# Weight sums of the seven-product down projection: from GpSimd to VectorE

## The chip, the cores and the metric

One core of a Trainium2 chip runs the whole kernel in one launch. The metric is the device time in microseconds (us), and lower is better. Five engines take part: TensorE (PE, with its weight loads as PEld), VectorE (DVE), ScalarE (ACT), GpSimd (POOL) and SyncE (SP), which issues the transfers.

## The reference, cut to what matters

The kernel computes a two-layer decoder trunk on 512 tokens of width 1024. Layer 0 has stick-breaking attention and layer 1 sliding-window attention. Each of them stands between two half-step SwiGLU blocks, so there are four SwiGLU blocks (stages 0, 1, 2 and 3), each with weights of its own:

```python
def swiglu(h, w_gate_up, w_down):
    gate, up = jnp.split(h @ w_gate_up, 2, axis=-1)
    return (jax.nn.silu(gate) * up) @ w_down

x = x + 0.5 * swiglu(rms_norm(x, norm_gains[i, 0]), ffn_w_gate_up[i, 0], ffn_w_down[i, 0])
```

The hidden width is 2816, which is 22 tiles of 128. Only the second product, with `w_down`, has to do with the change.

## The kernel before, in words

**Layout and precision.** Activations are kept transposed, as tiles of 128 features by 512 tokens. Every float32 operand of a matmul is split into a high and a low part (`hi`, `lo`), and each product is made of three matmuls. The weights come from HBM as float32 into `raw` buffers (two rings, three buffers in a feed-forward stage: `raw`, `raw`, `rawx`), issued by SyncE. They are split into `slot` buffers (four, each with room for 6 tiles of 128x128): ScalarE casts the high part (L282), VectorE subtracts to get the low part (L287).

**A feed-forward stage.** It has two halves, of 6 and of 5 pairs of hidden tiles (`PAIRED`). A half first makes its gate and up tiles (`gu`, 24 or 20 units of 24 matmuls with 512 columns), and `swiglu` turns each into the activation `h`. Then `down` multiplies these with the down weights.

**The seven products.** `down` works in 4 blocks. A block covers two output tiles (rows n and n+4) and takes the hidden tiles by even and odd, and the tokens by their two halves. A block is thus a 2x2 product of quarters, done with seven products in place of eight. The seven need sums of the activation quarters (`t`, L444 and L450 to L452 on VectorE, then split into `ops` at L435 and L436) and four sums of the weight quarters (`s`), which `make_sums` forms: s0 = a21+a22, s1 = s0-a11, s3 = a12-s1, s2 = a11-a21. Each has 128 rows and 6x128 or 5x128 columns. They are split like other weights (`slot<-s`). There is one buffer for each of s0 to s3, so a block's sum can't be written before the same sum of the block before has been split, and the two loads of the block must have landed.

**Order of the products.** For a block n it is 1, 5, (4 of block n-1), 2, 6, 3, 7, and the last block ends with 7, 3, 4. One product is 18 matmuls of 256 columns in the first half, and 15 in the second. The results gather in four PSUM banks (`dna` twice, `dnb`, `dnc`), and after each product VectorE adds the bank to the residual `x` (L542). Some products write again into the bank that the one before has left, so they wait for that addition. In the second half of stages 0 to 2 `norm_tile` follows on each output tile: casts and squares on ScalarE, `xl` on VectorE (L370), and the running sum of squares `acc` (L378), which GpSimd adds for 6 of 8 tiles.

**Order on the engines.** TensorE runs in the order of the program. On the other engines the compiler's scheduler sets a fixed order when the program is built: it plays the program through with its own estimates and takes, where several instructions are ready, the earlier one in the program. On the chip each engine then works strictly in that order. `pump` issues the next load as soon as a `raw` buffer is free, splits the next weights as soon as a slot is free, and calls `make_sums` when the first product of a block is next to be split, which is just behind the split for product 7 of the block before:

```python
        if column is not None and column not in self.sums:
            if self.fp and column + 1 < len(self.raws) and not self.unsplit:
                self.make_sums(column, t)
```

Of the kernel before, what the change touches and what calls it, by code (L numbers as in the profile page):

```python
# [131 lines left out]
class _Trunk:  # L132
# [76 lines left out]
    def make_sums(self, g, t):  # L209

        nc = self.nc
        a11, a12 = (self.raws[g][:, h * t * P : (h + 1) * t * P] for h in range(2))
        a21, a22 = (self.raws[g + 1][:, h * t * P : (h + 1) * t * P] for h in range(2))
        s = [self.fp.tile([P, SLOT], F32, tag=f"s{j}", name=f"s{j}_{g}", bufs=1)[:, : t * P] for j in range(4)]
        nc.gpsimd.tensor_add(s[0], a21, a22)  # L215
        nc.gpsimd.tensor_sub(s[1], s[0], a11)
        nc.gpsimd.tensor_sub(s[3], a12, s[1])
        nc.gpsimd.tensor_sub(s[2], a11, a21)
        self.sums[g] = s
        self.unsplit = 4  # L220
        self.reads[g] -= 1
        self.reads[g + 1] -= 1
# [1033 lines left out]
```

## Time and profile before

| | |
|---|---|
| median of 3 runs | 1956.06 us (1954.71 to 1960.08) |
| the profiled execution, its own time | 1953.03 us |
| its span in the profile | 1951.3 us |
| mean granted TensorE clock | 0.982 |
| PE busy | 1871.1 us |
| DVE busy | 1376.7 us |
| ACT busy | 830.7 us |
| POOL busy | 439.5 us |

In the views of the profile, times are in us from the start of the span unless marked ns. A row of the timeline has its start, its duration, the engine, the line of the kernel, the operation with output and inputs, the count, and in brackets the idle time ahead of it and what ended it. A row of the stretches has the stretch, its length, the busy time of PE, PEld, DVE, ACT and POOL with the counts of instructions, then the granted clock, the share of DMA time and the GB/s.

### The profile page before, as it was taken

The numbers are of one execution on the slowest core, as the hardware profiler recorded it, in microseconds if no ns is written. First come the engines' busy times: TensorE is split into PE (matmuls) and PEld (weight loads), VectorE is DVE, ScalarE is ACT, GpSimd is POOL, SyncE is SP. The second block draws the span as 40 slices with busy tenths as digits, with TensorE's granted clock in tenths as the row PEclk, the third lists the DMA queues.
The fourth block names the chain that finished last, engine by engine and source line by source line (L and its number), as shares of the span: only waits on it lengthen the run. The fifth ranks groups of instructions, "written<-read, shape, count | busy, mean of one in ns | idle before, by whom it ended". The sixth has DMA issues, their size and how long they took to land.

```text
span 1951.3 us, 26890 instructions
## 1 busy us (share of the span) xinstructions
PE 1871.1 (96%) x10578; PEld 1629.2 (83%) x10578; DVE 1376.7 (71%) x2208; ACT 830.7 (43%) x1384; POOL 439.5 (23%) x275
## 2 busy tenths in 40 slices
PE   9999999899999999999989999998999899999999
PEld 7889888877887888988888889888887788889889
DVE  6568557867887756856786577558877665685676
ACT  5333333456665433333343333334457543333332
POOL 1015002743321001500240033004242110131023
PEclk9999999999999999999999999998989999999999
DMA  5221322221112322132232223232210032222322
GB/s 173 98 95 68 122 95 81 89 69 56 42 65 71 114 97 97 67 120 97 72 105 97 95 73 111 95 99 76 88 60 28 18 123 97 98 80 97 105 71 98
DMA packets 36414, 170.78 MB, mean 88 GB/s; under 512 B 4416, under 2 KB 5184, under 8 KB 36288
## 3 DMA queue, kind: packets, MB, share of 16 engines
q1 hardware_dynamic: 36288, 169.07, 25.7%
q8 instruction: 83, 1.36, 0.3%
q14 instruction: 43, 0.35, 0.1%
HBM read 166.96 MB, written 2.10 MB: 87 GB/s over the span
## 4 chain that ended last, share of the span: by engine, by line
PE 80%; DVE 13%; ACT 3%; issue 3%; DMA 1%; POOL 0%; SPq 0%; ACTq 0%; DVEq 0%; POOLq 0%
PE gu L85 48%; PE dna L85 11%; PE dnc L85 4%; PE op L85 4%; DVE slot L287 4%; PE tok L85 3%; PE dnb L85 2%; PE pv L85 1%; DVE keep L640 1%; PE k L85 1%; DVE x L542 1%; DVE ops L436 1%; PE sc L85 1%; PE z L85 1%; ACT slot L282 1%
## 5 line engine op out<-in xcount | busy, mean ns | idle before, releaser
L85 PE MATMUL gu<-xh,slot 128*128 128x512 f32 x2800 | 868.2, 390 | 0.5 <-DVE slot L287 0.4
L85 PEld LDWEIGHTS gu<-xh,slot 128*128 128x128 f32 x2800 | 526.5, 188 | 112.1 <-DVE slot L287 2.1
L85 PE MATMUL gu<-xl,slot 128*128 128x512 f32 x1400 | 546.1, 390 | 2.1 <-DVE xl L370 2.1
L287 DVE TENSOR_TENSOR slot<-raw,slot 128x768 fp32r<-128x768 f32 (+2 forms) x270 | 288.1, 1068 | 165.1 <-ACT slot L282 162.7
L282 ACT CAST slot<-raw 128x768 fp32r<-128x768 f32 (+2 forms) x308 | 241.4, 785 | 363.9 <-PE gu L85 227.2
L85 PE MATMUL dna<-ops,slot 128*128 128x256 f32 x2112 | 284.4, 291 | 44.4 <-DVE x L542 31.4
L85 PEld LDWEIGHTS dna<-ops,slot 128*128 128x128 f32 x2112 | 271.8, 199 | 50.9 <-issue 25.5
L85 PEld LDWEIGHTS gu<-xl,slot 128*128 128x128 f32 x1400 | 263.5, 188 | 57.7 <-DVE xl L370 3.1
L215 POOL TENSOR_TENSOR s<-raw 128x768 f32<-128x768 f32 (+1 forms) x24 | 44.2, 1842 | 1047.0 <-DMA raw<-in_w_dram 991.6
L287 DVE TENSOR_TENSOR slot<-rawx,slot 128x768 fp32r<-128x768 f32 (+1 forms) x112 | 128.6, 1148 | 74.6 <-ACT slot L282 73.9
L282 ACT CAST slot<-s 128x768 fp32r<-128x768 f32 (+1 forms) x128 | 99.9, 781 | 145.4 <-PE dna L85 85.1
L287 DVE TENSOR_TENSOR slot<-s,slot 128x768 fp32r<-128x768 f32 (+1 forms) x128 | 143.4, 1120 | 24.3 <-ACT slot L282 23.5
L282 ACT CAST slot<-rawx 128x768 fp32r<-128x768 f32 (+1 forms) x112 | 87.0, 777 | 140.7 <-PE gu L85 78.4
L85 PE MATMUL dnc<-ops,slot 128*128 128x256 f32 x1056 | 141.4, 289 | 0.0
L85 PEld LDWEIGHTS dnc<-ops,slot 128*128 128x128 f32 x1056 | 135.7, 198 | 0.0
L285 POOL TENSOR_TENSOR slot<-raw,slot 128x384 fp32r<-128x384 f32 x76 | 91.7, 1233 | 139.5 <-ACT slot L282 139.5
L431 DVE TENSOR_TENSOR h<-gu,rbc 128x512 f32<-128x512 f32 x87 | 59.8, 688 | 83.5 <-PE gu L85 83.5
L85 PE MATMUL tok<-slot,xh 128*128 128x256 f32 x576 | 113.1, 295 | 0.2 <-POOL slot L285 0.2
L85 PEld LDWEIGHTS tok<-slot,xh 128*128 128x128 f32 x576 | 91.8, 196 | 3.1 <-issue 0.8
L430 ACT ACTIVATE g<-g 128x512 f32<-128x512 f32 x88 | 55.5, 631 | 86.6 <-DVE g L429 86.6
L435 ACT CAST ops<-h 128x256 fp32r<-128x256 f32 x88 | 45.2, 513 | 95.6 <-DVE h L432 95.6
L429 DVE TENSOR_TENSOR g<-gu,rbc 128x512 f32<-128x512 f32 x88 | 60.5, 687 | 35.9 <-PE gu L85 35.8
(303 smaller groups left out, 2503.5 us busy)
## 6 DMA issues: line engine op xcount, KB each, us to landing
raw<-in_w_dram SPq DMA_DIRECT2D x66, 768.0 KB, 4.3
raw<-in_w_dram SPq DMA_DIRECT2D x64, 640.0 KB, 3.9
rawx<-in_w_dram SPq DMA_DIRECT2D x28, 768.0 KB, 4.2
rawx<-in_w_dram SPq DMA_DIRECT2D x32, 640.0 KB, 3.9
raw<-in_ws_dram SPq DMA_DIRECT2D x20, 768.0 KB, 4.3
raw<-in_ww_dram SPq DMA_DIRECT2D x10, 768.0 KB, 4.2
x<-in_xt_dram SPq DMA_DIRECT2D x8, 256.0 KB, 5.6
out_dram<-x SPq DMA_DIRECT2D x8, 256.0 KB, 2.0
```

The lines of the kernel that those rows point to most:

```text
L85: return self._tc.keep_in_program_order(method(*args, **kwargs))
L215: nc.gpsimd.tensor_add(s[0], a21, a22)
L282: self.nc.scalar.copy(hi, src)
L285: self.nc.gpsimd.tensor_sub(lo[:, h], src[:, h], hi[:, h])
L287: self.nc.vector.tensor_sub(lo, src, hi)
L429: nc.vector.tensor_mul(g, gu[0], self.rbc)
L430: nc.scalar.activation(g, g, AF.Silu)
L431: nc.vector.tensor_mul(hf, gu[1], self.rbc)
L435: nc.scalar.copy(hi[:, a:b, :], src)
L436: nc.vector.tensor_sub(lo[:, a:b, :], src, hi[:, a:b, :])
L542: self.nc.vector.scalar_tensor_tensor(x, ps, 0.5, x, ALU.mult, ALU.add)
L640: nc.vector.tensor_tensor_scan(rev, rev, rev, 1.0, ALU.mult, ALU.bypass)
```

## The change

The four instructions of `make_sums` are issued to VectorE and not to GpSimd. Operands, shapes, buffers and their place in the program stay as they are.

```diff
-        nc.gpsimd.tensor_add(s[0], a21, a22)
-        nc.gpsimd.tensor_sub(s[1], s[0], a11)
-        nc.gpsimd.tensor_sub(s[3], a12, s[1])
-        nc.gpsimd.tensor_sub(s[2], a11, a21)
+        nc.vector.tensor_add(s[0], a21, a22)
+        nc.vector.tensor_sub(s[1], s[0], a11)
+        nc.vector.tensor_sub(s[3], a12, s[1])
+        nc.vector.tensor_sub(s[2], a11, a21)
```

There are 4 stages with 2 halves of 4 blocks, so `make_sums` runs 32 times and 128 instructions move.

## The prediction

> **What bounds the kernel now.** I read the page first, then the stretches of the eight down projections, then the timeline of one of them engine by engine, and at last who waits for whom.
>
> ```profile
> span 1951.3 us, 26890 instructions
> PE 1871.1 (96%) x10578; PEld 1629.2 (83%) x10578; DVE 1376.7 (71%) x2208; ACT 830.7 (43%) x1384; POOL 439.5 (23%) x275
> PE 80%; DVE 13%; ACT 3%; issue 3%; DMA 1%; POOL 0%; SPq 0%; ACTq 0%; DVEq 0%; POOLq 0%
> ```
>
> TensorE is the bound: busy for 96% of the span, 80% of the chain that ended last. GpSimd is on that chain with 0%, so nobody on the path waits for its results. What the change can win must come from VectorE's 13%. The next rows are stretches: first one gate and up phase, then the eight down projections from the first `dna` matmul to the next kind of matmul.
>
> ```profile
> 647.00:779.00 132.00, 132.00 (x587) 109.26 (x587) 87.85 (x178) 49.37 (x75) 9.62 (x4) 1.00 0.29 98
> ```
>
> ```profile
> 145.16:210.91 65.75, 61.16 (x505) 60.61 (x504) 54.65 (x62) 24.30 (x30) 27.05 (x12) 1.00 0.27 93
> 319.74:381.29 61.55, 53.31 (x421) 52.18 (x420) 54.17 (x65) 27.77 (x41) 34.52 (x21) 0.97 0.24 79
> ...
> 954.82:1019.17 64.35, 56.32 (x421) 54.84 (x420) 56.80 (x68) 29.27 (x44) 31.12 (x17) 0.92 0.25 78
> ...
> 1327.02:1390.88 63.86, 55.55 (x421) 54.66 (x420) 57.34 (x68) 29.41 (x44) 30.23 (x17) 0.92 0.24 78
> ...
> 1889.98:1947.67 57.69, 54.25 (x421) 53.22 (x419) 45.36 (x59) 19.34 (x27) 21.99 (x12) 0.94 0.25 88
> sum 513.05, PE 466.70 PEld 459.96 DVE 430.10 ACT 202.99 POOL 225.67; mean PE 58.34 PEld 57.49 DVE 53.76 ACT 25.37 POOL 28.21
> ```
>
> In the gate and up phase PE is busy all the time, with VectorE at two thirds. In the down projections PE idles 513.05 - 466.70 = 46.3 us. Of that the 5-pair halves have 8.2, 8.0, 8.3 and 3.4 us (length less PE busy), and the four 6-pair halves the rest, 18.3 us, 4.6 us each. The stretches are also the place where VectorE is nearly full: 57.34 of 63.86 us. Now one 6-pair half, VectorE first, then GpSimd, then PE.
>
> ```profile
> 148.17 2.07 DVE L450 TENSOR_TENSOR t<-h,t 128x256 f32<-128x256 f32 x1
> 150.16 2.06 DVE L451 TENSOR_TENSOR t<-h 128x256 f32<-128x256 f32 x1
> 152.15 0.41 DVE L452 TENSOR_TENSOR t<-h,t 128x256 f32<-128x256 f32 x1
> ...
> 153.68 0.94 DVE L436 TENSOR_TENSOR ops<-t,ops 128x768 fp32r<-128x768 f32 x1
> 154.55 0.41 DVE L542 SCALAR_TENSOR_TENSOR x<-dnc,x 128x256 f32<-128x256 f32 x1
> 154.89 2.27 DVE L287 TENSOR_TENSOR slot<-s,slot 128x768 fp32r<-128x768 f32 x1
> 157.08 0.41 DVE L542 SCALAR_TENSOR_TENSOR x<-dnb,x 128x256 f32<-128x256 f32 x1
> 157.41 2.44 DVE L287 TENSOR_TENSOR slot<-raw,slot 128x768 fp32r<-128x768 f32 x1
> 159.78 0.41 DVE L542 SCALAR_TENSOR_TENSOR x<-dna,x 128x256 f32<-128x256 f32 x1
> ```
>
> ```profile
> 147.60 2.35 POOL L215 TENSOR_TENSOR s<-rawx 128x768 f32<-128x768 f32 x1 [10.70 <-DMA rawx<-in_w_dram]
> 150.03 1.91 POOL L216 TENSOR_TENSOR s<-s,raw 128x768 f32<-128x768 f32 x1
> 153.90 2.44 POOL L217 TENSOR_TENSOR s<-raw,s 128x768 f32<-128x768 f32 x1 [1.96 <-DVE slot L287]
> 157.23 1.80 POOL L218 TENSOR_TENSOR s<-raw,rawx 128x768 f32<-128x768 f32 x1 [0.89 <-DVE slot L287]
> ```
>
> ```profile
> 152.95 2.41 PE L85 MATMUL dna<-ops,slot 128*128 128x256 f32 x18 [1.16 <-DVE x L542]
> 155.20 2.32 PE L85 MATMUL dnc<-ops,slot 128*128 128x256 f32 x18
> 160.34 1.90 PE L85 MATMUL dna<-ops,slot 128*128 128x256 f32 x14 [2.82 <-DVE x L542]
> ```
>
> Compare the two L450/L451 rows with L452, the same shape: 2.07 and 2.06 us against 0.41. They ran just while GpSimd ran a sum. Likewise the two splits of 2.27 and 2.44 against 0.94 for 768 columns. Only VectorE instructions with both inputs in SBUF are stretched; L542, which reads a bank, stays at 0.41 inside GpSimd's 153.90 to 156.34. So the two engines take turns, and GpSimd's sums hold VectorE up. PE stands for 1.16 and 2.82 us behind additions to `x` that stood in that queue.
>
> **What moves, and its price on VectorE.** 128 instructions leave GpSimd, half of 768 columns and half of 640. No transfer moves and SP's queue keeps its instructions. On VectorE the price is the step from one start to the next, since a next instruction starts before the row ends: 153.68 to 154.55 is 0.87 us for 768, and for 640 the rows below give 333.53 to 334.27, 0.74 us. A group of four costs 3.48 or 2.96 us, all 32 groups 16 x 3.48 + 16 x 2.96 = 103 us.
>
> The Trainium skill, VectorE: DVE Perf Modes, section on the TRN2 errata, gives a float32 tensor_tensor as (N+151)/0.96 ns, 957 and 824 ns here; by it all groups would cost 114 us. The rows of duration agree (0.94), but the steps are shorter, and I keep the steps.
>
> **Start of a 6-pair half.** What goes from VectorE's queue between 148.17 and 159.78: 1.66 + 1.65 (L450, L451 less 0.41) and 1.33 + 1.50 (splits less 0.94), 6.14 us. What comes is the group, 3.48 us. The chain to the addition that PE awaits gets 2.66 us shorter if all four sums stand ahead of it; if they fall into holes, both stalls go, 3.98 us at most. I take 3.3, nearer the middle since some of the sums will find holes while ScalarE makes casts: 4 x 3.3 = 13 us (10.6 to 15.9).
>
> **Start of a 5-pair half.**
>
> ```profile
> 331.14 2.14 DVE L287 TENSOR_TENSOR slot<-raw,slot 128x640 fp32r<-128x640 f32 x1
> ...
> 333.53 0.81 DVE L287 TENSOR_TENSOR slot<-s,slot 128x640 fp32r<-128x640 f32 x1
> 334.27 0.41 DVE L542 SCALAR_TENSOR_TENSOR x<-dnc,x 128x256 f32<-128x256 f32 x1
> ...
> 335.47 0.75 DVE L370 SCALAR_TENSOR_TENSOR xl<-x,gain,xh 128x512 fp32r<-128x512 f32 x1
> ...
> 349.72 1.78 DVE L370 SCALAR_TENSOR_TENSOR xl<-x,gain,xh 128x512 fp32r<-128x512 f32 x1
> ```
>
> Stage 3 has no norm behind it and idles 3.44 us, some 0.6 of it at its end (product 7 there follows 6 in one bank, which the change leaves). So its start costs 2.8, and I use this for all four. Lock waits here are 2.14 - 0.81 = 1.33 each; four of them less 2.96 leave 2.4. I take 4 x 2.4 = 10 us (6 to 11.2).
>
> **Later blocks of a 5-pair half, stages 0 to 2.** They idle 8.2 - 3.4 = 4.8 us more each, 14.4 together. Here `xl` (1.78 against 0.75, a wait of 1.03) and GpSimd's `acc` come in. Per block GpSimd holds VectorE up to six times, 6 x 1.2 (between 1.03 and 1.33) = 7.2 us; afterwards it is 2 x 1.03 + 2.96 = 5.0. That saves 2.2 us a block, but with VectorE this full it reaches PE only in part: 2 us a half, 6 together (0 to 12).
>
> **Slow matmuls behind the stalls.** From the chain of waits, in two halves:
>
> ```profile
> 160.34 4.54 PE dna L85 x36
> 164.88 2.16 PE dnc L85 x18
> ```
>
> ```profile
> 794.09 5.89 PE dna L85 x36
> ```
>
> 18 matmuls in 2.16 us are the normal pace, 0.12 each. The 36 behind a stall took 4.54 and 5.89 in place of 4.32. All 4 x (504 + 420) down matmuls at 0.12 make 443.5 us, and PE was occupied 466.7. These 23 us stand mostly behind stalls, in stretches with a granted clock of 0.92 to 0.97. With over half of the stalls gone I count 40%, 9 us (0 to 18); I don't take the full share, as two stalls of one length left such different tails.
>
> **What is late next: the loads.** From the view of L215, what ended GpSimd's idle time ahead of it (us, times):
>
> ```profile
>   DMA raw<-in_w_dram: 991.6, 18
> ```
>
> GpSimd came to its group early and sat until a load landed, 18 times by this view. GpSimd can afford it. In VectorE's queue a sum that stands there too early stops splits, activations and additions behind it, and PE behind these. The scheduler puts the sum where it estimates the landing; the trace of before can't show how good that is. Bounds: no wait, or a whole load, 4.3 us by the page's median below, per group.
>
> ```profile
> raw<-in_w_dram SPq DMA_DIRECT2D x66, 768.0 KB, 4.3
> ```
>
> A 6-pair block has 7 x 2.16 = 15.1 us of PE time, and VectorE's work then is 7 x (0.87 + 0.33) + 3.48 = 11.9, so 3.2 us are free. A 5-pair block has 12.6 against 7 x (0.74 + 0.33) + 2 x 0.75 + 2.96 = 12.0. I take a small wait, 0.3 us for each of the twelve later 5-pair groups: -4 us. The eight first groups of the halves lie in the gate and up phase, where VectorE has a third free: nothing, unless a wait there exceeds the lead of the four slots. Buffers come free no later, since the group ends earlier than GpSimd's 159.03.
>
> **The sum.** 13 + 10 + 6 + 9 - 4 = 34 us. Against the profiled execution's 1953.03 that is 1919; the median of the runs shown stands 3.0 us above it, so I predict 1956.06 - 34 = 1922 us.
>
> **Rivals.**
> *VectorE becomes the bound in the 5-pair halves.* With the `acc` waits, 12.0 + 2 x 1.03 = 14.1 us of work stand against 12.6 of PE. For: VectorE is at 57.34 of 63.86 already. Against: that figure contains waits that go. Then the later blocks win nothing, most slow tails stay, and the 5-pair starts win half: 13 + 5 - 2 = 16, 1940 us. The Trainium skill, Perfetto Trace Analysis, section Optimizing Scalar/DVE Operations, advises offloading a saturated VectorE even to GpSimd, which speaks for this rival, and adds that the shared port may spoil it, which speaks against; the rows above show the spoiling.
>
> *The sums wait for loads at the head of VectorE's queue: slower.* With a whole 4.3 us wait in 24 later groups, 6-pair blocks lose 4.3 - 3.2 = 1.1 and 5-pair blocks 4.3 - 0.6 = 3.7: 12 x 1.1 + 12 x 3.7 = 58, less the starts' 23, gives +35, 1991 us. It decides from a wait w with 12 (w - 0.6) > 23 + 6, that is about 3 us. For: most groups are gated by a load. Against: the scheduler counts some time for a load, and the start of a half has higher-ranked work to run first.
>
> *It is hidden anyway:* the order changes so that other additions to `x` come late and the stalls only move, within 6 us of 1956. Against: the lock waits on the chain exceed the sums at every place where PE stalled.
>
> **How the numbers follow.** The forecast (gain 20 to 50 us) has 0.60, a larger gain 0.04, VectorE as the bound (gain 6 to 20) 0.15, no change 0.09, slower by waits for loads 0.12. 0.3%, 5.9 us, is what a measurement of this kernel can tell, so faster 0.79, same 0.09, slower 0.12. The range 1898 to 1958 leaves out the slower rival and part of the largest gain; the forecast's own is 1906 to 1936.
>
> **What would show it.** Right: in the 6-pair halves PE's idle time falls from 4.6 to 0.6 to 2 us, L450 and L451 stand at 0.41 everywhere, splits of 768 columns at 0.94, the sums at about 0.95 and 0.82, and VectorE's total goes up by less than 103 us. The 5-pair halves of stages 0 to 2 fall from about 8 to 3 to 5 us of idle PE, and the clock there rises above 0.92. Wrong: VectorE idle for microseconds until a load ends ahead of L215, or PE waiting for `x` at more places than before.

## The result, and the profile after

The changed kernel takes 1939.76 us, the median of 4 runs (1937.73 to 1941.38), against 1955.6 for the kernel before (4 runs, 1954.71 to 1960.08). The ratio is 0.9914, with a 95% interval of 0.9896 to 0.9932: faster by 0.9%. That is inside the range of 1898 to 1958 us, but outside the 1906 to 1936 of the forecast itself, and less than half of the 34 us that were predicted. The page of its profile begins thus, with the shares of the chain as the third line here:

```profile
span 1935.8 us, 26732 instructions
...
PE 1865.5 (96%) x10578; PEld 1625.3 (84%) x10578; DVE 1342.6 (69%) x2336; ACT 833.8 (43%) x1384; POOL 174.8 (9%) x147
...
PE 77%; DVE 16%; ACT 3%; issue 2%; DMA 2%; POOL 0%; SPq 0%; ACTq 0%; DVEq 0%; POOLq 0%
```

VectorE took over 103 us of sums (the prediction's price) and is nevertheless busy for 34 us less: 1342.6 against 1376.7. So about 137 us of its busy time before (34 and 103) were waits for GpSimd. But VectorE's share of the chain went up, from 13% to 16%. The stretches of the down projections show where the gain stands (the 6-pair halves of stages 1 and 2 are left out):

```profile
145.01:208.51 63.50, 61.16 (x506) 60.63 (x505) 49.99 (x74) 24.38 (x30) 0.00 (x0) 1.00 0.29 97
317.33:379.38 62.05, 54.30 (x422) 53.57 (x420) 49.88 (x77) 29.27 (x43) 11.64 (x10) 0.94 0.23 78
...
949.08:1010.75 61.67, 54.27 (x422) 53.54 (x421) 52.60 (x80) 29.68 (x44) 7.64 (x5) 0.94 0.24 80
...
1315.09:1378.17 63.08, 55.68 (x421) 54.95 (x420) 52.16 (x80) 29.78 (x44) 7.63 (x5) 0.92 0.24 79
1702.40:1765.60 63.20, 61.02 (x505) 60.61 (x504) 50.09 (x74) 24.39 (x30) 0.00 (x0) 1.00 0.28 97
1874.43:1932.07 57.64, 52.97 (x421) 52.03 (x419) 42.58 (x71) 19.43 (x27) 0.00 (x0) 0.97 0.25 87
sum 498.26, PE 461.68 PEld 456.58 DVE 397.27 ACT 205.72 POOL 26.91; mean PE 57.71 PEld 57.07 DVE 49.66 ACT 25.71 POOL 3.36
```

The eight stretches shrank from 513.05 to 498.26, 14.8 us, nearly the whole change of the span (15.5). The four 5-pair halves sum to 244.4 us, against 247.5 before; the four 6-pair halves to 253.8 against 265.6. So the 6-pair halves gave 11.8 us and the 5-pair halves 3.0. PE's idle time fell from 46.3 to 36.6, its occupied time from 466.7 to 461.7. In the 5-pair halves PE still idles 7.8, 7.4, 7.4 and 4.7 us; in the last of them, that is 1.2 us more than before. This is VectorE at the start of a 6-pair half, and then PE:

```profile
148.01 0.42 DVE L450 TENSOR_TENSOR t<-h,t 128x256 f32<-128x256 f32 x1
148.35 0.41 DVE L451 TENSOR_TENSOR t<-h 128x256 f32<-128x256 f32 x1
...
152.29 0.95 DVE L215 TENSOR_TENSOR s<-rawx 128x768 f32<-128x768 f32 x1
153.16 0.95 DVE L218 TENSOR_TENSOR s<-raw,rawx 128x768 f32<-128x768 f32 x1
154.03 0.95 DVE L216 TENSOR_TENSOR s<-s,raw 128x768 f32<-128x768 f32 x1
154.90 0.41 DVE L542 SCALAR_TENSOR_TENSOR x<-dnb,x 128x256 f32<-128x256 f32 x1
155.23 0.95 DVE L217 TENSOR_TENSOR s<-raw,s 128x768 f32<-128x768 f32 x1
156.09 0.95 DVE L287 TENSOR_TENSOR slot<-raw,slot 128x768 fp32r<-128x768 f32 x1
156.96 0.41 DVE L542 SCALAR_TENSOR_TENSOR x<-dna,x 128x256 f32<-128x256 f32 x1
```

```profile
157.52 4.55 PE L85 MATMUL dna<-ops,slot 128*128 128x256 f32 x36 [1.56 <-DVE x L542]
```

The rows of 2 us are gone: L450 and L451 stand at 0.42 and 0.41, a sum at 0.95, and the steps from start to start are the 0.87 us of the prediction. Apart from the sums, VectorE's rows stand in the same order as before in all eight stretches. Both stalls have become one of 1.56 us. Its cause is in the same rows. PE waits for the addition at 156.96 (product 6's, whose bank product 7 writes again). Ahead of it stand the four sums, almost in one piece. In a 5-pair half the same picture:

```profile
324.31 0.81 DVE L215 TENSOR_TENSOR s<-rawx 128x640 f32<-128x640 f32 x1
325.04 0.81 DVE L218 TENSOR_TENSOR s<-raw,rawx 128x640 f32<-128x640 f32 x1
325.78 0.81 DVE L216 TENSOR_TENSOR s<-s,raw 128x640 f32<-128x640 f32 x1
326.51 0.41 DVE L542 SCALAR_TENSOR_TENSOR x<-dnb,x 128x256 f32<-128x256 f32 x1
326.85 0.81 DVE L217 TENSOR_TENSOR s<-raw,s 128x640 f32<-128x640 f32 x1
327.58 0.81 DVE L287 TENSOR_TENSOR slot<-raw,slot 128x640 fp32r<-128x640 f32 x1
328.31 0.41 DVE L542 SCALAR_TENSOR_TENSOR x<-dna,x 128x256 f32<-128x256 f32 x1
```

```profile
328.78 5.35 PE L85 MATMUL dna<-ops,slot 128*128 128x256 f32 x30 [2.29 <-DVE x L542]
345.17 3.82 PE L85 MATMUL dna<-ops,slot 128*128 128x256 f32 x30 [2.05 <-DVE x L542]
...
360.38 5.33 PE L85 MATMUL dna<-ops,slot 128*128 128x256 f32 x30 [2.40 <-DVE x L542]
```

One such stall stands in each of the first three blocks. Two of them are followed by 30 matmuls in 5.3 us, where a row of 30 without a stall takes 3.76 (shown below). Last, VectorE's waits for loads ahead of the sums, over the whole span (total, times, longest):

```profile
DVE s L215 <- DMA raw<-in_w_dram: 5.1, 10, 1.1
```

### The profile page after: what moved, and what is told of

Read it like the earlier page. It is cut to its first block, busy times and chain, and to the rows that moved or that the text cites. A ratio compares the mean times of both kernels' runs of the same rounds, so it can differ in the third digit from the quotient of the medians.

```text
span 1935.8 us, 26732 instructions
## 1 busy us (share of the span) xinstructions
PE 1865.5 (96%) x10578; PEld 1625.3 (84%) x10578; DVE 1342.6 (69%) x2336; ACT 833.8 (43%) x1384; POOL 174.8 (9%) x147
## 4 chain that ended last, share of the span: by engine, by line
PE 77%; DVE 16%; ACT 3%; issue 2%; DMA 2%; POOL 0%; SPq 0%; ACTq 0%; DVEq 0%; POOLq 0%
PE gu L85 48%; PE dna L85 10%; PE op L85 4%; PE dnc L85 3%; PE tok L85 3%; DVE slot L287 3%; DVE keep L640 2%; PE pv L85 1%; PE dnb L85 1%; DVE x L542 1%; DMA raw<-in_w_dram 1%; DVE s L216 1%; PE sc L85 1%; ACT slot L282 1%; DVE beta L641 1%
## 5 line engine op out<-in xcount | busy, mean ns | idle before, releaser
L287 DVE TENSOR_TENSOR slot<-raw,slot 128x768 fp32r<-128x768 f32 (+2 forms) x270 | 251.1, 931 | 156.9 <-ACT slot L282 154.5
L85 PE MATMUL dna<-ops,slot 128*128 128x256 f32 x2112 | 284.0, 292 | 36.6 <-DVE x L542 33.6
L287 DVE TENSOR_TENSOR slot<-rawx,slot 128x768 fp32r<-128x768 f32 (+1 forms) x112 | 99.8, 891 | 75.3 <-ACT slot L282 74.6
L378 POOL TENSOR_TENSOR acc<-acc,sq 128x512 f32<-128x512 f32 x30 | 44.9, 1496 | 1169.3 <-ACT sq L377 1169.3
L85 PE MATMUL dnc<-ops,slot 128*128 128x256 f32 x1056 | 137.1, 283 | 0.0
L287 DVE TENSOR_TENSOR slot<-s,slot 128x768 fp32r<-128x768 f32 (+1 forms) x128 | 113.5, 887 | 28.3 <-ACT slot L282 27.7
L85 PEld LDWEIGHTS dnc<-ops,slot 128*128 128x128 f32 x1056 | 131.3, 192 | 0.0
```

Of the source, the lines that this page charges most:

```text
L85: return self._tc.keep_in_program_order(method(*args, **kwargs))
L287: self.nc.vector.tensor_sub(lo, src, hi)
L378: (nc.gpsimd if done < POOL_SQUARES else nc.vector).tensor_add(self.acc, self.acc, sq)
```

## The experiments

The theory after this reading has two parts. The gain is that of the lock waits that left VectorE. A large part of it is given back, since the scheduler puts the group of sums ahead of the addition on which product 7 waits. The rivals: VectorE is full in the 5-pair halves in any order; the sums' waits for loads cost the rest; or the order alone does it, whatever the engine.

**Each half alone.** The engine is chosen by the number of pairs `t`.

```diff
-        nc = self.nc
+        nc = self.nc; eng = nc.vector if t == 6 else nc.gpsimd
-        nc.vector.tensor_add(s[0], a21, a22)
+        eng.tensor_add(s[0], a21, a22)
 ...
```

> Only the groups of the 6-pair halves (768 columns) are summed on VectorE; those of the 5-pair halves stay on GpSimd. Theory (the gain is the lock waits that left the start of the 6-pair halves; in the 5-pair halves the burst of four sums gives the gain back): the four 6-pair projections shorten by about 2.3 to 3.5 us each as in the changed kernel, 11.8 together, the 5-pair ones stay as before: 1943 to 1947 us. Rival (the gain is spread over all halves, as each GpSimd sum costs VectorE the same): half of it, 1947 to 1950 us.

Measured: 1939.25 us, ratio 0.9917 (0.9896 to 0.9939), faster than the 1943 to 1947 us expected. As a ratio it is the result of the full change, 0.9914. A 6-pair and a 5-pair half of it:

```profile
142.05:205.51 63.46, 61.15 (x505) 60.62 (x504) 49.99 (x74) 24.39 (x30) 0.00 (x0) 1.00 0.28 96
314.34:377.67 63.33, 55.17 (x422) 53.66 (x421) 54.55 (x66) 29.28 (x44) 35.64 (x22) 0.95 0.25 79
```

The 6-pair half is as in the changed kernel (63.50). This 5-pair half, with its sums on GpSimd, is 1.3 us longer than in the changed kernel and 1.8 longer than in the one before. But the four of them sum to 244.4 us, as in the changed kernel and 3.0 less than in the one before, although their sums run on GpSimd as they did there. So the 3.0 us that the 5-pair halves gave in the changed kernel can't be put down to the move of their sums; these halves differ by that much between kernels for other reasons.

> The other half of the split: only the groups of the 5-pair halves (640 columns) are summed on VectorE, those of 768 columns stay on GpSimd. Theory (there the burst of sums gives back what the lock waits cost): no more than 4 us from the kernel before. Rival (the two halves of the change help each other): 8 us or more faster.

Measured (with `t == 5`): 1954.07 us, ratio 0.9991 (0.9975 to 1.0008). The 5-pair groups on VectorE give nothing, as the theory expected; those halves sum to 246.1 us, against 247.5 before. The gain is that of the 6-pair groups alone.

**The sums ranked behind the addition.** `make_sums` waits until the addition of product 6 has been issued in the program. Nothing is added; only the rank changes by which the scheduler orders VectorE.

```diff
-            if self.fp and column + 1 < len(self.raws) and not self.unsplit:
+            if self.fp and column + 1 < len(self.raws) and not self.unsplit and not self.hold:
 ...
-        a = {}
+        a, self.hold = {}, True
 ...
-            self.used(slot, pairs)
+            self.hold = p != 6 and (n, p) != (BLOCKS - 1, 4); self.used(slot, pairs)
```

> Sums on VectorE, but their place in the program is moved behind the addition to x of product 6, so the scheduler ranks that addition above the four sums. Theory (the burst of four sums stands ahead of the addition that product 7 waits for): the waits of 1.56 us in the 6-pair halves and of 2.05 to 2.4 us in the 5-pair halves fall below 0.7 us, and with them go the slow matmuls behind: 1912 to 1925 us. Rival one (VectorE is full in the 5-pair halves, whatever its order): these keep over 10 us above the pace, only the 6-pair halves gain 1.5 us each: 1932 to 1938 us. Rival two (sums wait for loads): no change from the changed kernel, 1937 to 1942 us.

Measured: 1905.72 us (1903.73 to 1907.06), ratio 0.9749 (0.9729 to 0.9769), better than the theory's bounds. Of VectorE and PE at the place of the 2.29 us stall, and of the stretches (one 6-pair half, one 5-pair half, the sum of eight):

```profile
323.58 0.81 DVE L287 TENSOR_TENSOR slot<-raw,slot 128x640 fp32r<-128x640 f32 x1
324.32 0.41 DVE L542 SCALAR_TENSOR_TENSOR x<-dna,x 128x256 f32<-128x256 f32 x1
324.65 0.81 DVE L215 TENSOR_TENSOR s<-rawx 128x640 f32<-128x640 f32 x1
```

```profile
325.27 3.76 PE L85 MATMUL dna<-ops,slot 128*128 128x256 f32 x30
```

```profile
145.70:207.45 61.75, 60.90 (x505) 60.55 (x504) 49.71 (x74) 24.42 (x30) 0.00 (x0) 1.00 0.29 99
316.28:370.24 53.96, 51.13 (x422) 50.58 (x420) 47.51 (x77) 28.88 (x43) 13.32 (x10) 1.00 0.26 90
...
sum 464.91, PE 449.79 PEld 446.01 DVE 387.12 ACT 203.83 POOL 31.23; mean PE 56.22 PEld 55.75 DVE 48.39 ACT 25.48 POOL 3.90
```

The addition now stands ahead of the sums, product 7 starts without a wait, and the 5-pair half takes 53.96 in place of 62.05 us, with the same number of instructions on VectorE. So VectorE was not full there: that rival has fallen. In the 5-pair halves of stages 0 to 2 some other rows of VectorE have changed places too; in that of stage 3 only the sums have moved, and it takes 52.00 in place of 57.64 us. PE idles 15.1 us in the eight stretches and is occupied 449.8, only 6.3 above the pace of 443.5 (18.2 in the changed kernel, 23.2 before).

One stretch went the other way. The 6-pair half of stage 3 takes 64.99 us, against 63.20 in the changed kernel and 61.73 to 62.25 for the other three here. VectorE's row, and PE's behind it:

```profile
1713.53 0.96 DVE L215 TENSOR_TENSOR s<-raw 128x768 f32<-128x768 f32 x1 [2.76 <-DMA raw<-in_w_dram]
```

```profile
1718.77 6.03 PE L85 MATMUL dna<-ops,slot 128*128 128x256 f32 x36 [1.99 <-DVE x L542]
```

Here a sum stood at the head of VectorE's queue until its load landed, with product 6's addition behind it and behind two more sums. PE stood for 1.99 us, and the 36 matmuls after it took 6.03 us, where the first such row of this half takes 4.48. So the rival of the loads is real in this version, at some 3 us in one of eight projections. Over the whole span VectorE waits 13.7 us for loads ahead of L215, 2.8 at the longest, against 5.1 and 1.1 in the changed kernel.

**The same rank with the sums on GpSimd.** The three edits above, made to the kernel before.

> The same move behind product 6's addition, but with the sums on GpSimd as before. Theory (on GpSimd it is the lock that costs, and the sums then run at the same work of VectorE, a little later): within 8 us of the kernel before, 1948 to 1962 us, with VectorE's rows still stretched to 2 us and more. Rival (the order alone makes the gain, not the engine): 1930 us or less.

Measured: 1953.24 us, ratio 1.0003 (0.9984 to 1.0022). VectorE at the start of a 6-pair half:

```profile
146.97 2.07 DVE L450 TENSOR_TENSOR t<-h,t 128x256 f32<-128x256 f32 x1
148.96 2.07 DVE L451 TENSOR_TENSOR t<-h 128x256 f32<-128x256 f32 x1
150.95 0.41 DVE L452 TENSOR_TENSOR t<-h,t 128x256 f32<-128x256 f32 x1
```

The stretched rows are those of the kernel before, and so is the time. But the edit moved nothing: GpSimd's instructions and, in the eight projections, VectorE's stand in the order of the kernel before, since on GpSimd the sums have a queue of their own. So the rank gains nothing as long as the sums run on GpSimd, and another order with the sums there was not tested. Engine and rank are worth 2.5% together, 0.9% and nothing apart.

**Shorter locks.** In the kernel before, GpSimd sums only the first 128 columns of each quarter; the other columns of the sums are left out, in buffers that are cleared once in each stage.

```diff
-        nc.gpsimd.tensor_add(s[0], a21, a22)
+        nc.gpsimd.tensor_add(s[0][:, c], a21[:, c], a22[:, c])
 ...
```

> Sums on GpSimd, but only of the first 128 of 768 or 640 columns; the rest of the sums is left out (the buffers are cleared once per stage). It shows the time without long locks and without the sums on VectorE. Theory: each sum holds VectorE for 0.3 us or so, the waits in the 6-pair halves go but for the 0.6 us at the end, and in the 5-pair halves only those with the running sum of squares stay: 1908 to 1922 us, at or a little below the kernel that moves the sums behind product 6's addition. Rival (the stalls come from something else than the sums, such as the order of products or the loads): above 1940 us.

Measured: 1900.57 us, ratio 0.9721 (0.9694 to 0.9748), below the bounds expected. A sum, and the first two stretches:

```profile
145.27 0.52 POOL L216 TENSOR_TENSOR s<-s,raw 128x128 f32<-128x128 f32 x1
```

```profile
141.78:203.08 61.30, 60.69 (x506) 60.52 (x504) 42.13 (x62) 24.40 (x30) 6.65 (x12) 1.00 0.28 99
311.91:363.97 52.06, 50.99 (x422) 50.54 (x421) 42.62 (x66) 29.44 (x44) 18.50 (x22) 1.00 0.28 94
```

There are as many sums as before, on the same engine, and VectorE's rows stand in the same order in the projections; only the length of the sums has shrunk. (Some 3 us of the gain stand ahead of the first projection, which starts at 141.78 and not at 145.16. From 20 to 32 us the granted clock is 1.00 here and 0.76 in the kernel before. The run with only the 6-pair groups on VectorE has 1.00 there too and starts at 142.05, so these 3 us are not put down to the sums.) PE's idle time falls to 0.6 us in the 6-pair half and 1.1 in the 5-pair half. Over the whole span PE's waits for VectorE in the projections fall from 42.2 us (31.4 for additions to `x`, 10.8 for `ops`) to 3.0. That shows that the stalls of the kernel before came from the time that GpSimd held VectorE up. (The shorter sums are also ready sooner. In the kernel before ScalarE waited 10.7 us in all for sums, so little of the gain can lie there.) The Trainium skill, SBUF - State Buffer, section SBUF: two separate sides, states that the port pair of the two engines is taken for a whole instruction and that the loser blocks. The traces agree: an L450 of 0.41 us takes 2.07 beside a sum, and the additions that read a bank keep 0.41.

**The lock put back.** In the version with the sums behind the addition, GpSimd also does four subtractions of 512 columns for each group, into a buffer that nobody reads.

```diff
+        z = self.fp.tile([P, 4 * P], F32, tag="zz", name="zz", bufs=1)
+        [nc.gpsimd.tensor_sub(z, a[:, : 4 * P], b[:, : 4 * P]) for a, b in ((a21, a22), (a21, a11), (a12, a21), (a11, a21))]
```

> The version with the sums behind product 6's addition, and GpSimd does four subtractions of 512 columns more for each group, into a buffer that nobody reads. VectorE's own work stays the same; only the shared access is taken away from it 128 times, for some 1.0 to 1.2 us each. Theory (lock waits were the cost of the kernel before): a good part of the gain goes, 1920 to 1945 us, with VectorE rows stretched to about 2 us again. Rival (with the right order VectorE has room for the waits): 1903 to 1910 us.

Measured: 2006.66 us, ratio 1.0263 (1.0243 to 1.0282), far above the bounds. One group of VectorE, and the last of the same group on GpSimd:

```profile
149.46 1.72 DVE L287 TENSOR_TENSOR slot<-s,slot 128x768 fp32r<-128x768 f32 x1
151.10 0.41 DVE L542 SCALAR_TENSOR_TENSOR x<-dnb,x 128x256 f32<-128x256 f32 x1
...
153.07 2.01 DVE L215 TENSOR_TENSOR s<-rawx 128x768 f32<-128x768 f32 x1
```

```profile
152.41 3.81 POOL L218 TENSOR_TENSOR zz<-raw,rawx 128x512 f32<-128x512 f32 x2
```

The direction is the theory's, the size is not. VectorE's busy time in this run is 1459.5 us, 126 more than the 1333.2 of the version without the extra work, about 1.0 for each of the 128, and PE waits 88.8 us for additions to `x`, against 15.0 there. But the scheduler also ordered VectorE anew, and ScalarE now waits 70.9 us for sums, so how much of the 101 us is the lock alone is not settled by this run.

**No GpSimd in the down projections.** The version with the sums behind the addition, and the running squares on VectorE too (`POOL_SQUARES` from 6 to 0). This moves 30 additions, 5 in each of six norms, so more than those behind the three 5-pair halves. (In each norm GpSimd added for 5 of the 8 tiles, and not for 6, since the first tile needs no addition.)

> The version with the sums behind product 6's addition, with the running sum of squares also on VectorE for all tiles, so that GpSimd has no part in the down projections. VectorE gets 6 more additions of 512 columns (0.6 us from start to start) in each of three 5-pair halves and loses the last lock waits, 5 of some 0.7 us. Theory (VectorE is not full in the 5-pair halves once the order is right): within 4 us of that version, 1902 to 1909 us. Rival (VectorE is full there): 10 us or more slower.

Measured: 1897.2 us, ratio 0.9708 (0.9683 to 0.9733), better than the theory's bounds. The two versions were then run again side by side.

> The version with the sums on VectorE behind product 6's addition once more, beside the one that has the running squares on VectorE too, in more rounds on one chip. Theory: 0.975 of the kernel before, as in the first run (1904 to 1908 us there).

> As the version beside it, with the running sum of squares on VectorE for all tiles. Theory (the lock waits of the running squares are worth more than six additions of 0.6 us): 4 to 10 us faster than it. Rival (the difference of the first runs was chance): within 3 us of it.

Measured: 1907.7 us, ratio 0.9773 (0.9753 to 0.9793), as expected, and 1895.42 us, ratio 0.9722 (0.9697 to 0.9747). The difference is 12.3 us, more than the 4 to 10 expected, after 8.5 between the first runs, which were on two chips. So it was not chance, but only a small part of it is where the theory put it. The first `dna` matmuls of the two (first the one with the squares on GpSimd), and their sums over the eight projections:

```profile
144.76 2.32 PE L85 MATMUL dna<-ops,slot 128*128 128x256 f32 x18
```

```profile
139.44 2.31 PE L85 MATMUL dna<-ops,slot 128*128 128x256 f32 x18
```

```profile
sum 464.41, PE 449.79 PEld 445.99 DVE 387.76 ACT 204.43 POOL 31.28; mean PE 56.22 PEld 55.75 DVE 48.47 ACT 25.55 POOL 3.91
```

```profile
sum 460.45, PE 449.15 PEld 445.99 DVE 388.02 ACT 204.33 POOL 4.77; mean PE 56.14 PEld 55.75 DVE 48.50 ACT 25.54 POOL 0.60
```

5.3 us of the 12 stand ahead of the first projection, where the first norm runs, whose squares have moved too. There PE waits 0.80 and 1.32 us for `xl` in the one and 1.17 once in the other, and the granted clock from 20 to 32 us is 0.76 against 1.00. It was 1.00 in some runs with the squares on GpSimd as well, so what decides it stays open. 4.0 us are in the projections, 2.7 of them in the 6-pair half of stage 3 (64.97 against 62.30 us), which has no running squares. The 5-pair halves of stages 0 to 2, the theory's place, give 1.3 us. The rest lies outside the projections. VectorE takes more work and PE is no later for it, so the rival that VectorE is full has fallen once more. This is the best version of the study, 2.8% faster than the kernel before and some 2% faster than the changed one.

## Why the prediction was right or wrong

**Right: what bounds, and the sign.** The waits behind GpSimd's sums were the cost, and they went as read from the rows. 0.87 us a sum was measured again, and VectorE's total fell where the prediction only said that it would rise by less than 103 us. But one of its signs of being wrong came too: PE waited for `x` at 24 places, 22 before (33.6 us against 31.4). Nor did the 5-pair halves of stages 0 to 2 fall to 3 to 5 us of idle PE. In the eight stretches the parts of the 34 us came out as 9.0 at the 6-pair halves, 0.8 at the 5-pair halves and 5.0 from slow matmuls, 14.8 together.

**Start of a 6-pair half: a little below its range.** Predicted 13 us, with 10.6 if all four sums stand ahead of the awaited addition. They do. The stalls went from 1.16 + 2.82 to 1.56, 2.4 us a half. Over the four halves PE's idle time fell from 18.33 to 9.36 us, 9.0 together; with the slow matmuls, which the prediction counted apart, it makes the 11.8. The step that failed is the belief that some sums would fall into holes of VectorE's queue. Of several ready instructions the scheduler takes the earlier one in the program, and the group is issued ahead of product 6's addition.

**5-pair halves: the terms that failed.** Predicted 10 for the starts and 6 for later blocks; idle time there fell from 28.0 to 27.2 us, no more than it differs between kernels whose sums for these halves run on GpSimd (28.0 before, 29.2 with the 6-pair groups alone on VectorE). The prediction subtracted the group from the lock waits and took the rest as gain at PE. Both numbers were right, but they do not meet in the same place. PE in the 5-pair half of stage 0, kernel before:

```profile
330.20 0.50 PE L85 MATMUL dna<-ops,slot 128*128 128x256 f32 x2 [1.56 <-DVE ops L436]
...
333.66 3.86 PE L85 MATMUL dna<-ops,slot 128*128 128x256 f32 x30 [1.17 <-DVE x L542]
...
362.26 5.32 PE L85 MATMUL dna<-ops,slot 128*128 128x256 f32 x30 [2.85 <-DVE x L542]
```

Three of the four lock waits lay ahead of the activations. PE stood for these early in the half, 1.54 us and the 1.56 shown, and so only 1.17 us were left to wait at product 7. With the activations on time, PE comes to product 7 sooner and meets the group of 3.0 us: 4.3 us of stalls in the first block became 2.29. The second block had no such stall and got one of 2.05, and that of the third went from 2.85 to 2.40. So now each of the first three blocks has a stall of its own at product 7.

**Slow matmuls.** Predicted 9, measured 5.0 (466.7 to 461.7), since they go with the stalls and fewer of these went. The version with the addition ahead, where PE's idle time fell by 31 us, took 16.9 of the 23 us.

**Loads.** -4 us was set aside. VectorE waited for loads ahead of the sums for 5.1 us in all, 1.1 at the longest; what of this reached PE is not told apart. The rival that made the change slower needed about 3 us a group; it is refuted for this schedule. In the version with the addition ahead one such wait of 2.76 us did reach PE.

**The rival that hit the number.** VectorE as the bound of the 5-pair halves gave 1940 us, at a chance of 0.15, and 1939.76 came. Its mechanism is nevertheless wrong: with the same VectorE instructions in another order those halves are 5.6 to 9.1 us shorter each. Its number was right by luck: a right total is no proof of a reason. And that the measured time lies inside the wide range is no proof of the forecast, whose terms for the 5-pair halves came to almost nothing.

## What to carry to other kernels

When two engines hold each other up, price a move by what the one costs the other, not by the durations of the two: the sums cost VectorE 103 us and took some 137 us of waits off it. Then look where the moved work lands in the strict order of its new queue. A group of short instructions ahead of the one result that the bounding engine awaits gave back more than half of the gain here, since a stall that goes uncovers the next one in the same queue.

## What the runs showed of the hardware

- A GpSimd sum and a VectorE instruction with both inputs in SBUF take turns: beside a sum of 768 columns a VectorE row of 0.41 us takes 2.07 and ends some 0.3 us behind the sum (150.24 behind 149.95). An addition that reads a PSUM bank keeps its 0.41 us.
- Matmuls behind a PE stall of some 2 us can run at about 0.7 of their pace: 30 in 5.35 us where 3.76 is the row without a stall, in a stretch with a granted clock of 0.94. The length of the stall does not decide it: behind five stalls of 2.05 us in the changed kernel they took 3.82 twice and 5.31 three times. With the short sums, where no stall for an addition is over 0.6 us, the clock of all eight stretches was 1.00. What decides between the two tails stays open.
